# Entering the feed-forward sublayers: transposing four quarters and forming the three sums from the transposed blocks

## The chip, the core and the metric

The kernel runs on one core of one Trainium2 chip. The metric is the device time of one execution in microseconds. Three runs of the kernel before took 2835.72, 2828.82 and 2835.14 us, median 2835.14 us; a fourth execution was profiled.

## The reference, cut to what matters

A trunk of two layers on 512 tokens of width 1024; each layer is feed-forward, mixer (gated DeltaNet in the first, Mamba-2 in the second), cross-attention, feed-forward. So there are four feed-forward sublayers. What each does with the residual stream `h`:

```python
def swiglu(x, w_in, w_out):
    gate, up = jnp.split(x @ w_in, 2, axis=-1)
    return (jax.nn.silu(gate) * up) @ w_out

u = swiglu(rms_norm(h, g[0, 0]), ffn_w_in[l, 0], ffn_w_out[l, 0])
h = h + MACARON_W * rms_norm(u, g[0, 1])
```

All data are float32, `w_in` is 1024 x 5632, `w_out` 2816 x 1024.

## The kernel before, in words

**Arithmetic.** Every float32 operand of a product is split in two rounded parts, hi and lo (ScalarE casts hi, VectorE subtracts to get lo), and `mm3` (L143 to L145) issues three products: hi by hi, hi by lo, lo by hi. Features lie on partitions, tokens on the free axis, so what enters a sublayer must be transposed.

**The first product of a feed-forward** saves products by sums of quarters (seven instead of eight). With tokens cut in halves of 256 and features in halves of 512, the input is A11, A12 (first half of the tokens) and A21, A22. The products need A11, A12, A22 and S1 = A21 + A22, S2 = S1 - A11, S3 = A11 - A21, S4 = A12 - S2, each transposed and split in hi and lo. A11, A12, S1 and A22 go to the tiles `xh`/`xl`, the others to `s2h`/`s2l`, `s3h`/`s3l`, `s4h`/`s4l`.

**`FFN.enter(i, ...)`** (L365) does this for one block of 128 tokens, i = 0 to 3. VectorE scales the block with its reciprocal root and the gains (L373, two instructions of 128x512, into `u`). `put` then sends one 128x512 piece through TensorE's transpose (L379, four instructions of 128x128 into one PSUM bank), ScalarE casts hi out of the bank (L381) and VectorE subtracts lo (L382). For i = 0 and 1 there are two such pieces. For i = 2 and 3 there are five: x's second half for A22, and the sums `xs` (S1, L391), S2 (L394), S4 (L396) and S3 (L393), which VectorE forms from `u`, with tokens on partitions, before each is transposed. So one entry has 2 + 2 + 5 + 5 = 14 pieces and 56 transposes. The banks are those of tag "c", of which there are two (the first entry, at the kernel's start, also uses "s").

**What stands around it.** For the sublayer in front, `tail` finishes a block of 128 tokens, `post` (L225 multiplies by the gains `gbc`, L202 to L204 form the reciprocal root `rcol`, L230 adds to `h`), then `sumsq` (L196) and `enter` follow. After the last block's tail, `head` issues the products of the first four weight tiles with A11 and A12 (4 x 24 = 96 products of 128x256), which need only i = 0 and 1. `FFN.rest` goes on with `plain(0)` and `plain(1)`: two loads into `raw` (L440), T14 = their differences (L454, into the space of `h`), its split, products of the weights with S1, then of T14 with A22. `pair(2)` and on take the seven products; L489 and L492/L493 are its first operations on a `raw`. Tiles named `raw` have three buffers, so a load waits until an earlier `raw` has been read. `warm` loads ScalarE's table for Silu (L210).

**Order of the work.** The program is written out in plain order, and a scheduler orders each engine's instructions by priorities (`later` shifts them by a table, `LATER`); each engine then runs its own list strictly in that order. The list of each engine is known when the kernel is built.

The first entry stands at the kernel's start; the entry of FFN 1 comes after the first cross-attention, that of FFN 2 after FFN 1, that of FFN 3 after the second cross-attention. The instructions around the entries of FFN 1 and FFN 3 have the same order on VectorE and ScalarE.

Of the kernel before, what the change touches and what calls it, by code (L numbers as in the profile page):

```python
# [52 lines left out]
def prio(name):  # L53
    def wrap(f):
        def g(self, *a, **k):
            with getattr(self, "t", self).later(name):
                return f(self, *a, **k)
        return g
    return wrap
# [275 lines left out]
class FFN:  # L335
# [29 lines left out]
    @prio('ff_enter')  # L365
    def enter(self, i, ss, tag):

        t, nc = self.t, self.t.nc
        r = t.rcol(ss)
        x = t.u[:, i, :]  # L370
        a, b = slice(0, T), slice(T, D)
        for s in (a, b):
            nc.vector.scalar_tensor_tensor(x[:, s], t.h[:, i, s], r[:, 0:1], self.pg[:, s], op0=ALU.mult, op1=ALU.mult)  # L373
        ts = slice(i % 2 * P, i % 2 * P + P)

        def put(src, dst):
            ps = t.bank(tag)
            for k in range(4):
                nc.tensor.transpose(ps[:, k * P:k * P + P], src[:, k * P:k * P + P], t.cst(C_ID))  # L379
            p = ps.rearrange("p (k t) -> p k t", k=4)  # L380
            nc.scalar.copy(dst[0][:, :, ts], p)  # L381
            nc.vector.tensor_sub(dst[1][:, :, ts], p, dst[0][:, :, ts])  # L382

        if i < 2:
            put(x[:, a], self.A11)
            put(x[:, b], self.A12)
        else:
            y = t.u[:, i - 2, :]
            put(x[:, b], self.A22)
            s1 = t.nt.tile([P, T], F32, name="xs", bufs=2)  # L390
            nc.vector.tensor_add(s1, x[:, a], x[:, b])  # L391
            put(s1, self.S1)
            nc.vector.tensor_sub(x[:, a], y[:, a], x[:, a])  # L393
            nc.vector.tensor_sub(y[:, a], s1, y[:, a])  # L394
            put(y[:, a], self.S2)
            nc.vector.tensor_sub(y[:, b], y[:, b], y[:, a])  # L396
            put(y[:, b], self.S4)
            put(x[:, a], self.S3)
# [931 lines left out]
def run(t, phases, n0=0):  # L1330
# [17 lines left out]
    with ExitStack() as c:  # L1348
        if hasattr(phases[0], "gains"):
            phases[0].gains(c, n0)  # L1350
            phases[0].sums()
        for i in range(NT):
            if i:
                t.load(i)
            ss = t.nt.tile([P, 2], F32, name="ssh", bufs=2)
            for f in range(2):
                t.sumsq(t.h[:, i, f * T:f * T + T], ss[:, f:f + 1], f and i < 2)
            enter(i, n0, phases[0], ss, "cscc"[i])
            if i % 2:
                phases[0].head(i // 2, i == 1)  # L1360
        t.load_rest()
    for j, ph in enumerate(phases):
        n = n0 + j
        nxt = phases[j + 1] if j + 1 < len(phases) else None
        with ExitStack() as c:
            if hasattr(nxt, "gains"):
                nxt.gains(c, n + 1)
            ph.open(c)
            t.post_gain(n)
            t.warm(AF.Silu, t.xh[:, KB - 1, T - 1:T])  # L1370
            ph.rest()
            if hasattr(nxt, "sums"):
                nxt.sums()
            for i in range(NT):
                t.tail(ph, i)
                if i == 0:
                    t.warm(AF.Sqrt, t.ssu[:, 0, 0:1])
                if i == NT - 1:
                    c.close()
                    if nxt:  # L1380
                        nxt.head(0)
                ss = t.post(i, nxt)
                if nxt:
                    enter(i, n + 1, nxt, ss)
                else:
                    for f in range(2):
                        fs = slice(f * T, f * T + T)
                        nc.sync.dma_start(out=t.ap["out"][i * P:(i + 1) * P, fs], in_=t.h[:, i, fs])
            if nxt:
                nxt.head(1)  # L1390
# [41 lines left out]
```

## Time and profile before

| | |
|---|---|
| median of three runs | 2835.14 us (2828.82 to 2835.72) |
| the profiled execution, its own time | 2833.57 us |
| its span, first to last instruction | 2831.8 us |
| PE (TensorE) busy | 2785.9 us, 98% |
| DVE (VectorE) busy | 2071.3 us, 73% |
| ACT (ScalarE) busy | 1512.9 us, 53% |
| transposes of the entries (L379) | 224 instructions |
| granted TensorE clock, mean | 0.993 |

In the profile PE is TensorE's products (a transpose is one of them), DVE is VectorE, ACT ScalarE, SP the engine that issues the transfers. A row of a timeline has the start, the busy time, the engine, the line, the tile written and those read, and in brackets how long the engine had been idle and what released it. Busy times of neighbouring rows overlap, because engines are pipelined, so what an instruction takes from its engine is the distance between starts. The granted clock is a share of 2.4 GHz.

### The profile page before, as it was taken

What the parts mean: (1) busy time and instruction counts of PE and PEld (TensorE: products, weight loads), DVE (VectorE), ACT (ScalarE), POOL (GpSimd) and SP (SyncE); (2) the same over time, 40 slices, a digit from 0 to 9 for tenths busy, and PEclk for the clock granted to TensorE, in tenths of its full rate; (3) what the DMA queues carried; (4) which work ended last, traced back from release to release, by engine and by line L of the source; (5) the groups of instructions that cost most, each with busy time, mean ns of one, the idle gap of its engine ahead of it and who ended that gap; (6) DMA issues with size and microseconds to landing.
All of it is one profiled execution on the core that took longest, in us unless ns stands there. A gap on an engine that the chain in (4) does not pass through costs nothing.

```text
span 2831.8 us, 45624 instructions
## 1 busy us (share of the span) xinstructions
PE 2785.9 (98%) x17648; PEld 2453.5 (87%) x17648; DVE 2071.3 (73%) x4057; ACT 1512.9 (53%) x2814; POOL 124.5 (4%) x141
## 2 busy tenths in 40 slices
PE   8999999999999999999999999999999999999998
PEld 7999987788888887999988999888888888799997
DVE  8887777767666564887778887777667766588776
ACT  5444477666575574544445444576554656454433
POOL 0000001000000000000000000003212200000000
PEclk9999999999999999999999999999999999999999
DMA  6333433232323432433343332433233363233233
GB/s 215 106 105 105 160 111 103 62 100 81 94 71 121 168 116 73 143 100 102 97 156 127 98 112 90 152 121 108 85 104 106 103 217 112 75 113 112 93 109 105
DMA packets 125913, 320.71 MB, mean 113 GB/s; under 512 B 27472, under 2 KB 46672, under 8 KB 125184
## 3 DMA queue, kind: packets, MB, share of 16 engines
q1 hardware_dynamic: 125696, 317.80, 34.6%
q8 instruction: 139, 2.28, 0.3%
q14 instruction: 78, 0.64, 0.1%
HBM read 293.01 MB, written 24.74 MB: 112 GB/s over the span
## 4 chain that ended last, share of the span: by engine, by line
PE 86%; DVE 7%; ACT 3%; DMA 2%; issue 1%; SPq 0%; DVEq 0%; POOL 0%; ACTq 0%; POOLq 0%
PE ps_a L143 16%; PE ps_a L144 16%; PE ps_a L145 16%; PE ps_s L144 4%; PE ps_s L145 4%; PE ps_s L143 4%; PE ps_c L143 2%; PE ps_c L145 2%; PE ps_c L144 2%; PE ps_f L145 2%; PE ps_f L144 2%; PE ps_f L143 2%; DVE wlo L130 1%; PE ps_c L1068 1%; PE ps_s L1237 1%
## 5 line engine op out<-in xcount | busy, mean ns | idle before, releaser
L143 PE MATMUL ps_a<-xh,whi 128*128 128x256 f32 (+1 forms) x2368 | 754.8, 321 | 2.0 <-ACT xh L381 1.7
L144 PE MATMUL ps_a<-xl,whi 128*128 128x256 f32 (+1 forms) x2368 | 755.4, 320 | 0.1
L145 PE MATMUL ps_a<-xh,wlo 128*128 128x256 f32 (+1 forms) x2368 | 752.3, 319 | 0.0
L143 PEld LDWEIGHTS ps_a<-xh,whi 128*128 128x128 f32 x2368 | 453.5, 192 | 30.3 <-ACT xh L381 2.6
L144 PEld LDWEIGHTS ps_a<-xl,whi 128*128 128x128 f32 x2368 | 455.0, 192 | 26.4 <-DVE xl L382 0.5
L145 PEld LDWEIGHTS ps_a<-xh,wlo 128*128 128x128 f32 x2368 | 454.4, 192 | 23.9
L130 DVE TENSOR_TENSOR wlo<-raw,whi 128x1024 fp32r<-128x1024 f32 x278 | 339.8, 1224 | 159.2 <-ACT whi L129 157.2
L129 ACT CAST whi<-raw 128x1024 fp32r<-128x1024 f32 x278 | 289.1, 1043 | 224.5 <-PE ps_a L144 139.1
L137 ACT CAST whi<-h 128x1024 fp32r<-128x1024 f32 x168 | 175.6, 1048 | 204.3 <-PE ps_a L144 150.3
L138 DVE TENSOR_TENSOR wlo<-h,whi 128x1024 fp32r<-128x1024 f32 x168 | 205.3, 1224 | 88.7 <-ACT whi L137 87.7
L492 ACT CAST bh<-raw 128x512 fp32r<-128x512 f32 x80 | 49.7, 621 | 169.0 <-DMA raw<-ffn_in 140.5
L144 PE MATMUL ps_s<-wlo,hhi 128*128 128x512 f32 x352 | 138.0, 392 | 0.0
L143 PE MATMUL ps_s<-whi,hhi 128*128 128x512 f32 x352 | 137.8, 392 | 0.0
L145 PE MATMUL ps_s<-whi,hlo 128*128 128x512 f32 x352 | 137.2, 390 | 0.0
L143 PE MATMUL ps_c<-whi,hhi 128*128 128x512 f32 x288 | 112.0, 389 | 0.0
L144 PE MATMUL ps_c<-wlo,hhi 128*128 128x512 f32 x288 | 112.0, 389 | 0.0
L145 PE MATMUL ps_c<-whi,hlo 128*128 128x512 f32 x288 | 112.0, 389 | 0.0
L137 ACT CAST whi<-raw 128x1024 fp32r<-128x1024 f32 x80 | 84.0, 1051 | 50.3 <-PE ps_c L145 39.0
L485 DVE TENSOR_TENSOR h<-raw 128x512 f32<-128x512 f32 x80 | 55.1, 689 | 72.1 <-DMA raw<-ffn_in 69.4
L138 DVE TENSOR_TENSOR wlo<-raw,whi 128x1024 fp32r<-128x1024 f32 x80 | 97.4, 1218 | 8.7 <-ACT whi L137 8.7
L512 ACT ACTIVATE h<-h 128x512 f32<-128x512 f32 x80 | 50.6, 633 | 84.3 <-DVE h L509 84.1
L468 ACT CAST hhi<-h 128x512 fp32r<-128x512 f32 x88 | 54.8, 622 | 71.7 <-DVE h L513 43.6
(423 smaller groups left out, 6635.4 us busy)
## 6 DMA issues: line engine op xcount, KB each, us to landing
raw<-ffn_in SPq DMA_DIRECT2D x192, 512.0 KB, 4.2
raw<-ffn_out SPq DMA_DIRECT2D x88, 512.0 KB, 3.5
raw<-dn_in SPq DMA_DIRECT2D x48, 512.0 KB, 3.5
raw<-ssd_in SPq DMA_DIRECT2D x32, 512.0 KB, 3.5
hd<-h SPq DMA_DIRECT2D x24, 512.0 KB, 3.1
h<-hd SPq DMA_DIRECT2D x24, 512.0 KB, 4.2
raw<-dn_out SPq DMA_DIRECT2D x16, 512.0 KB, 3.6
raw<-xa_k SPq DMA_DIRECT2D x16, 512.0 KB, 3.9
```

The lines of the kernel that those rows point to most:

```text
L129: nc.scalar.copy(hi[:, :n], raw[:, :n])
L130: nc.vector.tensor_sub(lo[:, :n], raw[:, :n], hi[:, :n])
L137: nc.scalar.copy(hi, raw)
L138: nc.vector.tensor_sub(lo, raw, hi)
L143: mm(ps, lhs[0], rhs[0], start=first, stop=False)
L144: mm(ps, lhs[0], rhs[1], start=False, stop=False)
L145: mm(ps, lhs[1], rhs[0], start=False, stop=last)
L468: self.t.nc.scalar.copy(hi, x)
L485: sub(T1, u[:, a], g[:, a])
L492: nc.scalar.copy(b22[0], u[:, b])
L512: nc.scalar.activation(gt, gt, AF.Silu)
L1068: nc.tensor.matmul(py[:, e * 64:e * 64 + 64], st["gp"][e][:, c, :], st["xt"][:, c, e * 64:e * 64 + 64], start=True, stop=True)
```

## The change

`put` is cut in two: `turn` transposes one piece into a bank, `put` casts and subtracts from whatever it is given. For i = 0 and 1, ScalarE also copies each transposed piece back into `u`. For i = 2 and 3 only A22 and A21 are transposed, one behind the other; ScalarE copies A21 back into `u`, and the sums are formed from the transposed blocks and split from SBUF.

```diff
-        def put(src, dst):
+        def turn(src):
             ps = t.bank(tag)
             for k in range(4):
                 nc.tensor.transpose(ps[:, k * P:k * P + P], src[:, k * P:k * P + P], t.cst(C_ID))
-            p = ps.rearrange("p (k t) -> p k t", k=4)
+            return ps
+
+        def put(src, dst):
+            p = src.rearrange("p (k t) -> p k t", k=4)
             nc.scalar.copy(dst[0][:, :, ts], p)
             nc.vector.tensor_sub(dst[1][:, :, ts], p, dst[0][:, :, ts])
 
         if i < 2:
-            put(x[:, a], self.A11)
-            put(x[:, b], self.A12)
+            for s, dst in ((a, self.A11), (b, self.A12)):
+                ps = turn(x[:, s])
+                put(ps, dst)
+                nc.scalar.copy(x[:, s], ps)
         else:
             y = t.u[:, i - 2, :]
-            put(x[:, b], self.A22)
+            p22, p21 = turn(x[:, b]), turn(x[:, a])
+            put(p22, self.A22)
+            nc.scalar.copy(x[:, a], p21)
             s1 = t.nt.tile([P, T], F32, name="xs", bufs=2)
-            nc.vector.tensor_add(s1, x[:, a], x[:, b])
+            nc.vector.tensor_add(s1, p22, x[:, a])
             put(s1, self.S1)
             nc.vector.tensor_sub(x[:, a], y[:, a], x[:, a])
             nc.vector.tensor_sub(y[:, a], s1, y[:, a])
             put(y[:, a], self.S2)
```

In the changed file the cast of `put` is L384, its subtraction L385, the copies L391 (i = 0, 1) and L396 (A21), the sums L398 (S1), L400 (S3), L401 (S2), L403 (S4); lines behind `enter` are 7 higher (L454 is L461, L489 is L496, L492 is L499, L440 is L447). Outside the entries every engine's list is as before. Three places in the entry of FFN 1:

**TensorE**, from the last products of `head` (into `ps_s`) to the first of `plain(0)` (`ps_a<-xh` with four single rows is S1). Before:

```order
L144 MATMUL ps_s<-xl,whi 128x256
L379 MATMUL ps_c<-const,u 128x128 x4
L145 MATMUL ps_s<-xh,wlo 128x256
L143 MATMUL ps_a<-xh,whi 128x256 x2
L143 MATMUL ps_s<-xh,whi 128x256 x2
L379 MATMUL ps_c<-const,u 128x128 x4
L144 MATMUL ps_a<-xl,whi 128x256
L145 MATMUL ps_a<-xh,wlo 128x256
L379 MATMUL ps_c<-const,u 128x128 x4
```

Now:

```order
L144 MATMUL ps_s<-xl,whi 128x256
L145 MATMUL ps_s<-xh,wlo 128x256
L379 MATMUL ps_c<-const,u 128x128 x8
L143 MATMUL ps_a<-xh,whi 128x256 x2
L143 MATMUL ps_s<-xh,whi 128x256 x2
L144 MATMUL ps_a<-xl,whi 128x256
L145 MATMUL ps_a<-xh,wlo 128x256
```

Before, the transposes of i = 3 are spread over the last products of `head` and the first of `plain(0)`, and 14 rows stand between S1's and the product that needs them. Now all eight stand behind the last product of `head`, and the next instruction needs S1.

**VectorE**, from i = 2's last sums to i = 3's scaling (L373; `s4l` and `s3l` are i = 2's, `rcol`, L230 and what follows i = 3's). Before:

```order
L382 TENSOR_TENSOR s4l<-ps_c,s4h 128x4x128
L204 RECIPROCAL rcol<-rcol 128x1
L138 TENSOR_TENSOR wlo<-h,whi 128x1024
L382 TENSOR_TENSOR s3l<-ps_c,s3h 128x4x128
L230 SCALAR_TENSOR_TENSOR h<-u,rcol,h 128x512 x2
L454 TENSOR_TENSOR h<-raw 128x512 x2
L202 TENSOR_TENSOR rcol<-ssh 128x1
L204 RECIPROCAL rcol<-rcol 128x1
L373 SCALAR_TENSOR_TENSOR u<-h,rcol,pg 128x512 x2
```

Now:

```order
L385 TENSOR_TENSOR s4l<-u,s4h 128x4x128
L202 TENSOR_TENSOR rcol<-ssu 128x1
L461 TENSOR_TENSOR h<-raw 128x512
L204 RECIPROCAL rcol<-rcol 128x1
L461 TENSOR_TENSOR h<-raw 128x512
L230 SCALAR_TENSOR_TENSOR h<-u,rcol,h 128x512 x2
L202 TENSOR_TENSOR rcol<-ssh 128x1
L496 TENSOR_TENSOR h<-raw 128x512
L204 RECIPROCAL rcol<-rcol 128x1
L373 SCALAR_TENSOR_TENSOR u<-h,rcol,pg 128x512 x2
```

The two subtractions on the loads of `plain(1)` (L454, now L461) moved ahead of L230, and `pair(2)`'s first subtraction on a load (L489, now L496) moved from behind i = 3's scaling to ahead of it.

**ScalarE and SP** in the same entry; on ScalarE from i = 3's `rcol` to the cast of S1. Before:

```order
L203 ACTIVATE rcol<-rcol,eps 128x1
L381 CAST xh<-ps_c 128x4x128
L210 ACT_TABLE_LOAD
L210 ACTIVATE warm<-xh 128x1
L381 CAST xh<-ps_c 128x4x128
```

Now:

```order
L203 ACTIVATE rcol<-rcol,eps 128x1
L499 CAST bh<-raw 128x512
L384 CAST xh<-ps_c 128x4x128
L396 COPY u<-ps_c 128x512
L210 ACT_TABLE_LOAD
L210 ACTIVATE warm<-xh 128x1
L384 CAST xh<-xs 128x4x128
```

On SP the loads of `plain` and `pair`, before:

```order
L440 DMA raw<-ffn_in 128x1024 x4
L214 DMA gbc<-post 128x1024
L1339 DMA hd<-h 128x1024
L440 DMA raw<-ffn_in 128x1024
L356 DMA pg<-pre 128x1024
L128 DMA raw<-ffn_out 128x1024
```

Now:

```order
L447 DMA raw<-ffn_in 128x1024 x4
L214 DMA gbc<-post 128x1024
L447 DMA raw<-ffn_in 128x1024
L128 DMA raw<-ffn_out 128x1024
L1346 DMA hd<-h 128x1024
L356 DMA pg<-pre 128x1024
```

The cast of S1 now has the copy of A21 and the table load between it and A22's cast, and `pair(2)`'s cast on a load (L499) in front of both; on SP the spill of `h` stands behind `pair(2)`'s load and the first load of `w_out`.

## Rows read from the trace of the kernel before

**Rows 1.** The page: busy time of the engines, and the chain that ended last.
```profile
PE 2785.9 (98%) x17648; PEld 2453.5 (87%) x17648; DVE 2071.3 (73%) x4057; ACT 1512.9 (53%) x2814; POOL 124.5 (4%) x141
...
PE 86%; DVE 7%; ACT 3%; DMA 2%; issue 1%; SPq 0%; DVEq 0%; POOL 0%; ACTq 0%; POOLq 0%
```

**Rows 2.** Timeline of PE, one piece's transposes among products, entry of FFN 2.
```profile
1490.92 0.28 PE L143 MATMUL ps_a<-xh,whi 128*128 128x256 f32 x1
1491.04 0.60 PE L379 MATMUL ps_c<-const,u 128*128 128x128 f32 x4
1491.40 0.36 PE L144 MATMUL ps_a<-xl,whi 128*128 128x256 f32 x1
1491.60 0.28 PE L145 MATMUL ps_a<-xh,wlo 128*128 128x256 f32 x1
```

**Rows 3.** Timeline of PE, entry of FFN 1, from the first product of head.
```profile
1134.86 0.28 PE L143 MATMUL ps_a<-xh,whi 128*128 128x256 f32 x1
...
1147.25 0.63 PE L379 MATMUL ps_c<-const,u 128*128 128x128 f32 x4 [0.42 <-DVE u L373]
...
1150.56 0.49 PE L143 MATMUL ps_a<-xh,whi 128*128 128x256 f32 x2
...
1151.68 0.66 PE L379 MATMUL ps_c<-const,u 128*128 128x128 f32 x4 [0.40 <-DVE xl L382]
...
1152.78 0.36 PE L143 MATMUL ps_a<-xh,whi 128*128 128x256 f32 x1
```

**Rows 4.** Timeline of DVE, the same entry, from plain(0)'s second L454 to i = 3's L373.
```profile
1134.50 0.69 DVE L454 TENSOR_TENSOR h<-raw 128x512 f32<-128x512 f32 x1 [0.72 <-DMA raw<-ffn_in]
...
1140.31 1.20 DVE L138 TENSOR_TENSOR wlo<-h,whi 128x1024 fp32r<-128x1024 f32 x1
1141.43 0.68 DVE L382 TENSOR_TENSOR s3l<-ps_c,s3h 128x512 fp32r<-128x512 f32 x1
1142.03 1.40 DVE L230 SCALAR_TENSOR_TENSOR h<-u,rcol,h 128x512 f32<-128x512 f32 x2
...
1145.69 1.42 DVE L373 SCALAR_TENSOR_TENSOR u<-h,rcol,pg 128x512 f32<-128x512 f32 x2
```

**Rows 5.** Timeline of ACT, the same entry, i = 3's casts of A22 and S1.
```profile
1147.91 0.59 ACT L381 CAST xh<-ps_c 128x512 fp32r<-128x512 f32 x1 [2.46 <-PE ps_c L379]
1148.52 1.28 ACT L210 ACT_TABLE_LOAD   x1
...
1149.92 0.57 ACT L381 CAST xh<-ps_c 128x512 fp32r<-128x512 f32 x1
```

**Rows 6.** A load of pair(2) in FFN 2's entry: issue, landing; the slowest 512 KB loads' median.
```profile
1502.44 0.33 SPq L440 DMA_DIRECT2D raw<-ffn_in  x1
...
1506.66 0.62 ACT L492 CAST bh<-raw 128x512 fp32r<-128x512 f32 x1 [0.86 <-DMA raw<-ffn_in]
...
h<-x SPq DMA_DIRECT2D x4, 512.0 KB, 5.6
```

**Rows 7.** Timeline of PE, entry of FFN 2, i = 3.
```profile
1504.55 0.63 PE L379 MATMUL ps_c<-const,u 128*128 128x128 f32 x4 [3.40 <-DVE u L373]
...
1507.82 0.80 PE L143 MATMUL ps_a<-xh,whi 128*128 128x256 f32 x2 [1.74 <-ACT xh L381]
...
1510.01 0.41 PE L145 MATMUL ps_a<-xh,wlo 128*128 128x256 f32 x1
1510.22 0.41 PE L143 MATMUL ps_a<-xh,whi 128*128 128x256 f32 x1
...
1513.43 0.28 PE L143 MATMUL ps_a<-xh,whi 128*128 128x256 f32 x1
```

**Rows 8.** A stretch of PE: us, busy (instructions), granted clock, DMA share, GB/s.
```profile
1508.00:1514.00 6.00, 6.00 (x34) 0.63 0.00 0
```

**Rows 9.** Timelines of DVE and PE, the first entry.
```profile
14.29 1.42 DVE L373 SCALAR_TENSOR_TENSOR u<-h,rcol,pg 128x512 f32<-128x512 f32 x2
...
33.95 0.50 PE L143 MATMUL ps_a<-xh,whi 128*128 128x256 f32 x2
```

## The prediction

> **What bounds the kernel now.** The page comes first: PE is busy for 98% of the span and the chain that ended last lies on PE for 86% [rows 1]. So a product less is time less, as long as PE does not end up waiting. That is asked where the change acts, in the four entries, about 20 us each. The order of reading there: the timeline of PE (what a transpose costs, where PE waits), then the chain that ends PE's wait, followed back through ScalarE and VectorE, then the clock.
>
> One piece's four transposes, among products that start 0.12 us apart, push the next product from 0.12 to 0.36 us behind and the one after it from 0.12 to 0.20 or so: 0.44 us for a piece [rows 2]. In the entry of FFN 1, `head`'s 96 products begin at 1134.86, S1's first product starts at 1150.56 [rows 3]. Of these 15.7 us the products take 96 x 0.12 = 11.5, six pieces' transposes 6 x 0.44 = 2.6, waits on VectorE most of the rest. In the same 15.7 us block i = 3 goes through `post`, `sumsq` and `enter`, on VectorE and ScalarE, and becomes S1 only at its end: S1's cast starts at 1149.92 and takes 0.57 [rows 5], PE takes S1 at once. So here **two things end together, PE's list and the chain of block i = 3**, and the transposes fill time in which PE would have waited. In the entry of FFN 2 the chain is already the longer one: PE waits 3.40 and 1.74 us in it, and its clock falls [rows 7, 8].
>
> **The change, part by part.**
>
> *Removed:* 6 of 14 pieces in an entry, 24 in all, 24 x 0.44 = 10.6 us of PE. Per entry the three sums of i = 2 and the three of i = 3, so 6 x 0.44 = 2.6 us, and all of them stand in or just behind the stretch in which the chain of i = 3 runs.
>
> *Added:* six copies of 128x512 from PSUM on ScalarE per entry, 0.5 us from start to start like a cast [rows 5]; casts from SBUF instead of PSUM (bounds 0.57 and 0.62 us, L381 and L492 [rows 5, 6]: no difference that matters). VectorE has as many instructions as before, 0.60 us from start to start [rows 4]. Off the chain all this is free, because ScalarE is busy for 53% only [rows 1].
>
> *Moved, and here the price lies.* I walk the queues in their new order with the distances of the rows.
>
> Entry of FFN 1. VectorE before: from L454 at 1134.50 to i = 3's L230 at 1142.03 [rows 4]. Now between the same two stand thirteen instructions of 0.60 (that L454 included), one L138 of 1.1 and two small ones of 0.1, 9.1 us: L230 at 1143.6. The two extra ones are `plain(1)`'s L461s, which moved ahead; the first of them, which ends at 1142.9, also gives its `raw` buffer back, and only then SP can issue `pair(2)`'s load. The same load in the next entry landed 4.2 us after its issue [rows 6]: here at 1147.1. VectorE's L496 waits for it, and **behind L496 stand i = 3's reciprocal and its L373**, so L373 starts at 1147.1 + 0.6 + 0.1 = 1147.8, not 1145.69 [rows 4], and the transposes at 1149.35, not 1147.25 [rows 3]. PE, with three pieces fewer of i = 2 and no waits, is through `head` at 1134.9 + 11.5 = 1146.4 and waits 3.0 us. After the transposes (8 of them, 0.75 us) ScalarE casts A22 0.66 us behind their start, as before [rows 3, 5], copies A21 (0.5), loads the Silu table (1.4 up to the next row [rows 5]) and casts S1 (0.6): 1150.0 + 0.5 + 0.5 + 1.4 + 0.6 = 1153.0. The sum on VectorE is done under the table load. So S1's product starts at 1153.0 instead of 1150.56, **2.4 us later**, behind a second wait of 2.9 us.
>
> From there PE gets back what the old list had behind S1: two pieces (0.9) and a wait of 0.40 [rows 3]. The twentieth product behind S1 came at 1154.3 (the one at 1152.78 is the seventh [rows 3], thirteen more at 0.12). At full clock it would now come at 1153.0 + 19 x 0.12 + 0.2 (S1's lo) = 1155.5: +1.2. But two waits of 3.40 and 1.74 us, with 0.7 us of transposes between, brought the clock to a mean of 0.63 in FFN 2's entry, that is to 1.2 of 2.4 GHz for about 4.4 of 6 us [rows 7, 8]; products then start 0.21 apart [rows 7]. With waits of 3.0 and 2.9 I take the same here: 1153.0 + 19 x 0.21 = 1157.0, **+2.7**. The Trainium skill (TensorE: Matmul & The Clock Gate, section on HAM oscillation) says that waits between bursts of products let the clock fall and that the next burst starts at half rate; the trace agrees in FFN 2's entry, and by that rule the entry costs 2.7, without it 1.2.
>
> Entry of FFN 3: the same order on VectorE and ScalarE, +2.7.
>
> Entry of FFN 2. Two copies of i = 1 (1.0) and an L461 (0.6) now stand ahead of i = 2's reciprocal; i = 2's L373 comes 1.3 later, the L461 that frees the load's buffer 0.7 later, so the load lands at 1507.3 instead of 1506.66 [rows 6]. ScalarE's L499 waits for it, and the copy of A21, the table load and S1's cast stand behind: 1507.3 + 0.5 + 0.5 + 1.4 + 0.6 = 1510.3 instead of 1507.82 [rows 7]. Both are at the low clock. The twentieth product came at 1513.7 (the one at 1513.43 is the eighteenth [rows 7]), with three pieces ahead of it; now at 1510.3 + 19 x 0.21 = 1514.3: **+0.6**.
>
> First entry. Two copies stand ahead of the first weights' cast, whose subtraction stands ahead of i = 1's reciprocal on VectorE: L373 1.0 later than 14.29, PE's start with it. Through VectorE's longer list S1 is ready at 35.0 instead of 33.95 [rows 9], and three pieces behind it (1.3) come back: **-0.2**.
>
> Sum: -0.2 + 2.7 + 0.6 + 2.7 = **+5.8 us**. Against the profiled execution's own time, 2833.6, that is 2839.4; the median of the runs shown is 1.6 higher, so 2841.0 as a median. Bounds: if the clock does not fall in FFN 1 and 3, -3.0 (then +2.8); if the load lands at once L373 still waits for the chain through ScalarE, -0.4 in three entries; if it lands in 5.6 us, the slowest of the loads of its size [rows 6], +1.4 in three entries, +10.0 in all. I take 4.2, from the same load in the nearest entry.
>
> **The rivals.** About 0.3%, 8.5 us, is what a measurement of this kernel can tell from no change.
>
> *The chain is no longer than before* (its waits hide each other): S1 at its old times, and only the pieces behind S1 come back: 0.9 + 0.4 in FFN 1 and 3, 1.3 in the first entry, three pieces in FFN 2, two of them at half clock, 2.2: -6.1, 2829.0. For it speaks that ScalarE and VectorE have idle time in between; against it that VectorE's list ahead of L230 is counted longer by two instructions and has hardly a gap [rows 4].
>
> *PE is the bound throughout* and all 24 pieces come off: -10.6, 2824.5. For it: 98% [rows 1]. Against: the waits of rows 7, and that S1's transposes were ready early only because they were spread. It decides if S1 is ready before `head`'s 96 products end.
>
> *The loads land late.* On SP `pair(2)`'s load is now followed at once by a load of `w_out`, where the spill of `h` stood; two loads share the engines and hold up VectorE in front of L496. With 5.6 us: +10.0, 2845.1, over 0.3%; it decides from 0.9 us more than the 4.2 on.
>
> **How the numbers follow.** The forecast (+0.5 to +8.5) 0.58, the unlengthened chain 0.13, the full gain 0.07, late loads or a longer chain beyond +8.5 0.22. So faster 0.07, same 0.71, slower 0.22. The likeliest time is 2841.0; the range reaches down past the second case (2829.0) and up past the third rival (2845.1), each by a little for the spread of the runs shown: 2828 to 2849.
>
> **What would show it.** Right: 128 transposes, no wait of PE for anything but the entries; in FFN 1 and 3 a wait of about 3 us on L373 ahead of eight transposes, a second of about 3 us on the cast of S1 (L384), then products 0.21 apart; VectorE idle ahead of L496 on a load; PE's busy time lower and its idle time higher by more. Wrong: transposes of i = 3 that start at the old time after the tail, clock at 1.00 in FFN 1, or PE's idle time unchanged, which would mean that the 24 pieces were paid out.

## The result, and the profile after

The changed kernel took **2852.2 us** in the median of its runs (2849.1 to 2854.6), the kernel before 2834.3 beside it: ratio **1.0066, 95% interval 1.0048 to 1.0085**, so 13.6 to 24.1 us slower. Forecast were 2841.0 and a range of 2828 to 2849. The profiled execution took 2854.3 us, its span 2852.5: 20.7 over the span of before.

The page after, busy time [against rows 1]:

```profile
PE 2786.5 (98%) x17552; PEld 2452.9 (86%) x17552; DVE 2073.1 (73%) x4057; ACT 1527.1 (54%) x2838; POOL 128.0 (4%) x141
```

PE runs 96 instructions less, which are the 24 pieces, and is busy for as long as before: what the pieces gave back, instructions at the low clock took (the mean granted clock went from 0.993 to 0.987). PE's idle time rose by 20.1 us. Much of it shows in the group of PE's transposes (after the bar: busy time and mean, then the idle time ahead and what ended it), before:

```profile
L379 PE MATMUL ps_c<-const,u 128*128 128x128 f32 x184 | 29.8, 289 | 16.7 <-DVE u L373 14.8 <-DVE u L394 0.9 <-DVE xl L382 0.8
```

and after:

```profile
L379 PE MATMUL ps_c<-const,u 128*128 128x128 f32 x120 | 19.9, 308 | 26.4 <-DVE u L373 26.2
```

Before, this group waited 14.8 us for L373, and now 26.2. The wait of the first product of S1 (L143) for its cast, 1.7 us in one place before, is 8.2 in three.

**Where the 20.7 us arose.** Lines behind `enter` are 7 higher now, but the instructions of ScalarE are the same ones, so their shift between the two traces can be read. Two of them ahead of and behind the entry of FFN 1, before:

```profile
1093.99 1.28 ACT L210 ACT_TABLE_LOAD   x1
...
1232.67 0.63 ACT L512 ACTIVATE h<-h 128x512 f32<-128x512 f32 x1 [1.11 <-DVE h L509]
```

and the same two after:

```profile
1104.79 1.28 ACT L210 ACT_TABLE_LOAD   x1
...
1247.91 0.64 ACT L519 ACTIVATE h<-h 128x512 f32<-128x512 f32 x1 [1.11 <-DVE h L516]
```

The shift is 10.80 ahead and 15.24 behind: this entry cost 4.4 us. An entry's cost is this difference: the shift behind it less the shift ahead of it. With medians over all ScalarE instructions of a stretch ahead and behind, every run of this study gives such a row (us, against the profile of before; "elsewhere" is the shift at the end less the four entries):

| kernel | first | FFN 1 | FFN 2 | FFN 3 | sum | elsewhere |
|---|---|---|---|---|---|---|
| the change | 1.85 | 4.45 | 0.98 | 5.66 | 12.9 | 7.8 |
| the change, once more | 1.81 | 5.51 | -0.01 | 6.11 | 13.4 | 10.4 |
| first entry only | 1.66 | -0.01 | 0.02 | -0.54 | 1.1 | 2.0 |
| FFN 1 to 3 only | -0.18 | 5.66 | 1.34 | 5.68 | 12.5 | -4.4 |
| L496 tied | 0.64 | 3.93 | 0.13 | 3.45 | 8.2 | 12.7 |
| fillers | 1.02 | 3.37 | -2.12 | 3.76 | 6.0 | 10.1 |
| i = 0 and 2 only | 2.81 | 6.07 | -0.91 | 6.32 | 14.3 | 0.8 |
| i = 1 and 3 only | 4.39 | -0.34 | 1.28 | -0.39 | 4.9 | 0.1 |
| L496 tied, short chain | 0.11 | 1.37 | -0.44 | 1.00 | 2.0 | -3.4 |
| the same with fillers | 0.01 | 1.82 | -0.26 | 0.69 | 2.3 | 2.6 |
| the same, i = 2's rest removed | 4.52 | -0.87 | -0.10 | -1.44 | 2.1 | 1.6 |
| what paid, together | -0.52 | -1.20 | -0.33 | -1.93 | -4.0 | 0.4 |

Entries that a kernel left as they were cost -0.5 to 0.0, so this measure is good to about half a us. The entries of the change itself differ by up to 1.1 us between its two profiles, so smaller differences between two kernels say little. "Elsewhere" isn't a term of the entries. In the change, 5.8 of its 7.8 us arise at 858 to 868 us, deep in DeltaNet, where PE's granted clock was at its lower level (columns: busy us of PE, PEld, DVE, ACT and POOL with their instructions, granted clock, DMA share, GB/s):

```profile
860.00:870.00 10.00, 10.00 (x58) 8.08 (x57) 3.72 (x20) 6.57 (x23) 0.00 (x0) 0.50 0.01 2
```

and before:

```profile
860.00:870.00 10.00, 10.00 (x59) 8.75 (x59) 8.87 (x28) 6.51 (x14) 1.27 (x2) 1.00 0.64 173
```

Such stretches come and go in all kernels of the table. If the lost clock is added up over rows of 10 us from 450 to 1085 us (10 x (1 - clock) each), it is 13.7 us in the profile of before, 20.5 in that of the change, 27.2 with L496 tied, 6.8 with the short chain: 6.8, 13.5 and -6.9 against before, where the table has 7.8, 12.7 and -3.4. In the other kernels of the table the two numbers also agree within 4 us (8.4 against 10.4 in the second profile of the change).

**Inside the entry of FFN 1.** Take the shift ahead of the entry, 10.8, off these times to compare them with [rows 3 to 5]; times so reduced are called times on the old scale below. VectorE:

```profile
1154.20 1.41 DVE L230 SCALAR_TENSOR_TENSOR h<-u,rcol,h 128x512 f32<-128x512 f32 x2
1156.56 0.16 DVE L202 TENSOR_TENSOR rcol<-ssh 128x1 f32<-128x1 f32 x1 [0.94 <-ACT junk L196]
1159.37 0.69 DVE L496 TENSOR_TENSOR h<-raw 128x512 f32<-128x512 f32 x1 [2.66 <-DMA raw<-ffn_in]
1159.98 0.16 DVE L204 RECIPROCAL rcol<-rcol 128x1 f32<-128x1 f32 x1
1160.17 1.41 DVE L373 SCALAR_TENSOR_TENSOR u<-h,rcol,pg 128x512 f32<-128x512 f32 x2
```

L230 comes 1.4 us later than before (1143.4 against 1142.03). Then VectorE stands 2.66 us idle at L496 for its load, with the last block's L204 and L373 behind it. SP's queue, to see when that load was issued:

```profile
1153.65 0.33 SPq L447 DMA_DIRECT2D raw<-ffn_in  x1
1154.31 0.33 SPq L128 DMA_DIRECT2D raw<-ffn_out  x1
1155.64 0.33 SPq L1346 DMA_DIRECT2D hd<-h  x1
```

From the issue at 1153.65 to L496 at 1159.37 are 5.7 us, with a second load and the spill of `h` (`hd`) directly behind, and the load of the gains `gbc` (L214, at 1152.38) directly ahead. ScalarE:

```profile
1157.84 0.28 ACT L203 ACTIVATE rcol<-rcol,eps 128x1 f32<-128x1 f32 x1
...
1162.40 0.59 ACT L384 CAST xh<-ps_c 128x512 fp32r<-128x512 f32 x1 [2.41 <-PE ps_c L379]
1163.13 0.59 ACT L396 COPY u<-ps_c 128x512 f32<-128x512 f32 x1
1163.73 1.28 ACT L210 ACT_TABLE_LOAD   x1
1165.13 0.60 ACT L384 CAST xh<-xs 128x512 fp32r<-128x512 f32 x1
```

The square root (L203) had been done at 1158.1, so L496 cost 1.9 us of the chain. The four rows below it on ScalarE are A22's cast, A21's copy, the table and S1's cast, in the order that the prediction walked. PE:

```profile
1145.51 0.27 PE L143 MATMUL ps_a<-xh,whi 128*128 128x256 f32 x1
...
1156.89 0.28 PE L145 MATMUL ps_s<-xh,wlo 128*128 128x256 f32 x1
1161.73 1.36 PE L379 MATMUL ps_c<-const,u 128*128 128x128 f32 x8 [4.56 <-DVE u L373]
1165.79 0.80 PE L143 MATMUL ps_a<-xh,whi 128*128 128x256 f32 x2 [2.70 <-ACT xh L384]
...
1167.02 0.41 PE L145 MATMUL ps_a<-xh,wlo 128*128 128x256 f32 x1
1167.23 0.41 PE L143 MATMUL ps_a<-xh,whi 128*128 128x256 f32 x1
...
1169.29 0.28 PE L145 MATMUL ps_a<-xh,wlo 128*128 128x256 f32 x1
1169.41 0.28 PE L143 MATMUL ps_a<-xh,whi 128*128 128x256 f32 x1
```

`head`'s 96 products run through (11.5 us), then PE waits 4.56 and 2.70 us, with eight transposes between. Products behind S1 start 0.21 apart until 1169.3, then 0.12. The clock of the same stretch:

```profile
1158.00:1160.00 2.00, 0.00 (x0) 0.00 (x0) 0.63 (x2) 0.74 (x2) 0.00 (x0) 1.00 1.00 397
...
1162.00:1164.00 2.00, 1.09 (x8) 0.69 (x6) 1.14 (x3) 1.44 (x3) 0.00 (x0) 0.59 0.66 225
...
1166.00:1168.00 2.00, 2.00 (x10) 2.00 (x11) 2.00 (x4) 1.40 (x3) 0.00 (x0) 0.50 0.00 0
...
1170.00:1172.00 2.00, 2.00 (x19) 2.00 (x18) 1.71 (x2) 1.28 (x2) 0.00 (x0) 1.00 0.00 0
```

PE did nothing at 1158 to 1160, the clock fell behind that, to 1.2 of 2.4 GHz, and rose again once S1's products ran. Before, it stayed at 1.00 in this entry, also where S1's products begin:

```profile
1150.00:1152.00 2.00, 1.60 (x13) 1.37 (x13) 2.00 (x4) 1.50 (x4) 0.00 (x0) 1.00 0.79 303
```

In FFN 2 and FFN 3 PE shows the same two waits [against rows 7]:

```profile
1519.99 1.94 PE L379 MATMUL ps_c<-const,u 128*128 128x128 f32 x8 [4.84 <-DVE u L373]
1524.78 0.79 PE L143 MATMUL ps_a<-xh,whi 128*128 128x256 f32 x2 [2.85 <-ACT xh L384]
...
2505.21 1.94 PE L379 MATMUL ps_c<-const,u 128*128 128x128 f32 x8 [4.51 <-DVE u L373]
2509.85 0.80 PE L143 MATMUL ps_a<-xh,whi 128*128 128x256 f32 x2 [2.70 <-ACT xh L384]
```

The first entry [against rows 9]. PE began block i = 1 so before the change:

```profile
15.10 1.97 PE L379 MATMUL ps_s<-const,u 128*128 128x128 f32 x8 [4.35 <-DVE u L373]
```

Now it starts 1.34 us later, then waits for the last block and, in `pair(2)`, for the split of a load (L500):

```profile
16.44 1.97 PE L379 MATMUL ps_s<-const,u 128*128 128x128 f32 x8 [5.33 <-DVE u L373]
...
31.81 1.06 PE L379 MATMUL ps_c<-const,u 128*128 128x128 f32 x8 [1.64 <-DVE u L373]
...
52.27 0.39 PE L145 MATMUL ps_a<-s4h,bl 128*128 128x256 f32 x1 [0.96 <-DVE bl L500]
```

Before, PE had neither of the last two waits.

### The profile page after: what moved, and what is told of

It reads as the page before. It is cut to its first block, busy times and chain, and to the rows that moved or that the text cites. A ratio compares the mean times of both kernels' runs of the same rounds, so it can differ in the third digit from the quotient of the medians.

```text
span 2852.5 us, 45440 instructions
## 1 busy us (share of the span) xinstructions
PE 2786.5 (98%) x17552; PEld 2452.9 (86%) x17552; DVE 2073.1 (73%) x4057; ACT 1527.1 (54%) x2838; POOL 128.0 (4%) x141
## 4 chain that ended last, share of the span: by engine, by line
PE 86%; DVE 7%; DMA 3%; ACT 2%; issue 1%; POOL 0%; SPq 0%; DVEq 0%; ACTq 0%
PE ps_a L143 16%; PE ps_a L145 16%; PE ps_a L144 16%; PE ps_s L144 4%; PE ps_s L143 4%; PE ps_s L145 4%; PE ps_c L145 2%; PE ps_c L143 2%; PE ps_c L144 2%; PE ps_f L145 2%; PE ps_f L144 2%; PE ps_f L143 2%; DMA raw<-ffn_in 1%; DVE wlo L130 1%; PE ps_c L1075 1%
## 5 line engine op out<-in xcount | busy, mean ns | idle before, releaser
L143 PE MATMUL ps_a<-xh,whi 128*128 128x256 f32 (+1 forms) x2368 | 757.6, 322 | 8.3 <-ACT xh L384 8.2
L143 PEld LDWEIGHTS ps_a<-xh,whi 128*128 128x128 f32 x2368 | 456.0, 193 | 37.5 <-ACT xh L384 9.7
L499 ACT CAST bh<-raw 128x512 fp32r<-128x512 f32 x80 | 49.8, 622 | 174.8 <-DMA raw<-ffn_in 135.5
L143 PE MATMUL ps_s<-whi,hhi 128*128 128x512 f32 x352 | 137.8, 392 | 0.0
L143 PE MATMUL ps_c<-whi,hhi 128*128 128x512 f32 x288 | 112.0, 389 | 0.0
L492 DVE TENSOR_TENSOR h<-raw 128x512 f32<-128x512 f32 x80 | 55.2, 690 | 75.1 <-DMA raw<-ffn_in 73.4
```

Of the source, the lines that this page charges most:

```text
L143: mm(ps, lhs[0], rhs[0], start=first, stop=False)
L492: sub(T1, u[:, a], g[:, a])
L499: nc.scalar.copy(b22[0], u[:, b])
```

## The experiments

**One part of the entries at a time.** The new and the old way side by side in `enter`, chosen by

```diff
+        new = self.idx == 0
+        if not new:
...
+            return
```

> The new way of forming the sums in the first entry alone; the entries of FFN 1, 2 and 3 as before. In the profiles of the changed kernel and of before the first entry cost 1.85 us, FFN 1's 4.3, FFN 2's 1.0, FFN 3's 5.65 (12.8 in all), and 7.8 us arose elsewhere, 5.8 of them in one stretch of low granted clock at 858 to 868 us, far from any entry. Theory A (the cost lies in the entries, and what arose elsewhere is no part of the mechanism): +1.9 us against the kernel before, about 2836, granted clock 0.993. Theory B (the new first entry shifts what follows, and the rest of the kernel pays): +1.9 + 7.8 = +9.7, about 2844, with a low clock near 860.

Measured: ratio 1.0004 (0.9985 to 1.0023), and 1.1 us in the entries. 9.7 us would be 1.0034, outside the interval: theory B falls, although this profile too has a low clock at 860 to 870.

With `new = self.idx > 0`:

> The first entry as before, the new way in FFN 1, 2 and 3. Up to 1104 us this is the kernel before, instruction for instruction. Theory A: +4.3 + 1.0 + 5.65 = +11.0, about 2845, and whether the stretch of low clock near 860 appears is chance (then about 5.8 more). Theory B: +11.0 and never a low clock near 860, which the shift by the first entry had caused; together with the run of the first entry alone the two differences make up the +18 of the changed kernel.

Measured: ratio 1.0037 (1.0020 to 1.0054), 5.7 to 15.3 us; by the trace 12.7 in the three entries. The stretch of low clock at 850 to 870 us is there without the new first entry: that entry isn't its cause.

**The subtraction in front of the last block**

```diff
+        if n == 2:
+            nc.vector.tensor_copy(T3[:, 0:1], self.S1[1][:, 0, 255:256])
         sub(T3, u[:, b], u[:, a])
```

> The changed kernel with pair(2)'s subtraction for T3 (L496) tied behind the low half of S1, by a tiny copy of 128x1, so that it can't stand ahead of the last block's reciprocal and L373 on VectorE. In the profile of the changed kernel L496 waited 2.66 us for its load in FFN 1 and 2.31 in FFN 3 with the reciprocal ready behind it. Theory A (this wait is a term of the chain): L373 and S1's first product 1.9 us earlier in FFN 1 and 3, little in FFN 2, so -3 to -4 against the changed kernel, about 2848.5. Theory C (the chain through ScalarE and the clock set S1 anyway): within 1 us of the changed kernel, about 2852.

Ratio to before 1.0043 (1.0026 to 1.0061). VectorE in FFN 1 (its shift ahead of the entry is 14.4 here):

```profile
1161.50 0.16 DVE L204 RECIPROCAL rcol<-rcol 128x1 f32<-128x1 f32 x1 [1.25 <-ACT rcol L203]
1161.69 1.42 DVE L373 SCALAR_TENSOR_TENSOR u<-h,rcol,pg 128x512 f32<-128x512 f32 x2
```

and PE:

```profile
1163.26 1.93 PE L379 MATMUL ps_c<-const,u 128*128 128x128 f32 x8 [2.56 <-DVE u L373]
1167.88 0.80 PE L143 MATMUL ps_a<-xh,whi 128*128 128x256 f32 x2 [2.70 <-ACT xh L384]
```

L373 starts at 1147.3 on the old scale instead of 1149.4: 2 us, as theory A has it, and PE's first wait falls from 4.56 to 2.56. The entries cost 4.8 less than in the change (5.3 against its second profile), of it 2.2 to 2.7 in FFN 3 and 1.2 in the first entry, where I had expected none; in FFN 1 only 0.5 to 1.6, since the clock fell there all the same, and stayed low until 5.5 us behind S1's first product, in the change 3.5. What is left of the first wait comes from ScalarE: L204 waits for L203 (1161.18), which stands behind L216 (1160.22, the halving of the gains).

**The clock.** `fill` issues products of A11 or A22 with themselves, at a late priority, into banks that the transposes and S1's product overwrite, so they fill the waits and change no result:

```diff
+            p22, p21 = turn(x[:, b], 36 * k), turn(x[:, a], k)
...
+        if n == 0 and self.idx:
+            self.fill(ps[0][:, 256:], self.A22, 20)
         for i in range(2):
             self.product(ps[i][:, 256:], self.part(ws[i], 0), self.S1, True, False)
```

> The changed kernel with 37 filler products ahead of the last block's transposes and 20 ahead of S1's first product, in FFN 1, 2 and 3; their sums are thrown away. PE waited 4.5 to 4.8 and 2.7 to 2.9 us there, and its granted clock was 0.50 from the end of the first wait until 3.6 (FFN 1), 6.7 (FFN 2) and 4.1 us (FFN 3) behind S1's first product. Theory A (the waits let the clock fall, and the products behind S1 pay): clock 1.00 in the entries, S1's products 0.12 apart and not 0.21, half of those times back, 1.8 + 3.3 + 2.0 = -7 against the changed kernel, about 2845; S1's first product not earlier by more than 0.5 us. Rival (the low clock has another cause): the clock stays low, and no time comes back or some is lost.

Ratio to before 1.0045 (1.0030 to 1.0060). The three entries by stretches:

```profile
1157.00:1171.00 14.00, 13.17 (x106) 12.53 (x106) 8.86 (x15) 8.47 (x15) 0.00 (x0) 1.00 0.38 137
1514.00:1532.00 18.00, 17.15 (x138) 16.29 (x137) 16.18 (x26) 11.64 (x21) 0.00 (x0) 1.00 0.27 89
2497.00:2511.00 14.00, 13.17 (x106) 12.48 (x105) 8.89 (x15) 8.32 (x15) 0.00 (x0) 1.00 0.28 98
```

The clock stays at 1.00 in all three, and they cost 6.1 less than in the change (6.6 against its second profile); expected were 7. So with the waits filled the clock doesn't fall, and that is worth about 2 us an entry. The Trainium skill (TensorE: Matmul & The Clock Gate, section on HAM oscillation) has it that waits between bursts bring the clock down; these rows agree, with the reverse: filled waits keep it up.

**Which half of the rows.** `new = i % 2 == 0` and `new = i % 2 == 1`, in all four entries:

> The new way for the blocks i = 0 and 2 alone; i = 1 and 3 as before, in all four entries. In VectorE's list of FFN 1 and 3 the subtraction for T3 still stands ahead of the last block's reciprocal. An entry's cost is read as the shift, against the kernel before, of the work behind it less that of the work ahead of it. Theory A (the longer list of i = 2 and the late load are the larger half): PE waits about 4 us ahead of the last block's transposes in FFN 1 and 3, and each costs 3 to 4 us, FFN 2 about 0. Theory D (what costs is the last block's own chain, through the copy of A21 and the sum): at most 0.5 us each.

> The new way for the blocks i = 1 and 3 alone; i = 0 and 2 as before. VectorE's list up to the last block's L373 is that of before, and the subtraction for T3 stands behind the sum for S1. Theory A: no wait of PE over 0.5 us ahead of the eight transposes, then one of 2.7 us on S1's cast, clock 1.00 in FFN 1 and 3; these two cost 1 to 1.5 us each. Theory D: 3 us or more each.

With i = 0 and 2 alone (single execution, 2848.7 us), VectorE and PE in FFN 1:

```profile
1152.87 0.69 DVE L522 TENSOR_TENSOR h<-raw 128x512 f32<-128x512 f32 x1 [2.77 <-DMA raw<-ffn_in]
```

```profile
1155.23 1.09 PE L390 MATMUL ps_c<-const,u 128*128 128x128 f32 x4 [5.11 <-DVE u L373]
```

L522 is L496 here. With i = 1 and 3 alone (single execution, 2838.6 us), PE:

```profile
1152.54 1.06 PE L379 MATMUL ps_c<-const,u 128*128 128x128 f32 x8 [0.41 <-DVE u L373]
...
1156.35 0.50 PE L143 MATMUL ps_a<-xh,whi 128*128 128x256 f32 x2 [0.96 <-ACT xh L384]
```

Theory D falls: the longer chain of i = 3 costs nothing in FFN 1 and 3 (-0.3 and -0.4), because L373 is nearly on time (1146.1 on the old scale, before 1145.69), PE takes the transposes ahead of `head`'s last 15 products and these cover all but 0.96 us of the chain. The half of i = 2 carries all of it, and more (6.1 and 6.3). Theory A had the side right and both sizes wrong. In the first entry it is the other way round (4.4 for i = 1 and 3, 2.8 for i = 0 and 2), which I hadn't expected; the clock fell there in both (0.88 at 40 to 50 us, 0.83 at 30 to 40), while it stayed at 1.00 in the change, so the halves don't add up to the whole.

**The chain of the last block, shortened,** on top of the tied L496:

```diff
-            p22, p21 = turn(x[:, b]), turn(x[:, a])
-            put(p22, self.A22)
+            p21 = turn(x[:, a])
             nc.scalar.copy(x[:, a], p21)
+            p22 = turn(x[:, b])
...
             put(s1, self.S1)
+            put(p22, self.A22)
...
-            t.warm(AF.Silu, t.xh[:, KB - 1, T - 1:T])
+            k = 4 if isinstance(ph, FFN) else KB
+            t.warm(AF.Silu, t.xh[:, k - 1, T - 1:T])
```

> The kernel with L496 tied behind S1's low half, and besides A21 turned and copied ahead of A22, S1's cast ahead of A22's, and the load of the Silu table put behind S1's cast. In the profile of that kernel PE waited 2.56 us on L373 and 2.70 on S1's cast in FFN 1. Theory A (the rest is the chain from the transposes to S1): the second wait falls by the cast (0.5) and what of the table load was on the path (0.7), to 1.2 to 1.7 us, and an entry costs 1.0 to 1.5 us less than with L496 tied alone (3.9, 0.1 and 3.5). Rival (VectorE, not ScalarE, sets S1): the second wait stays over 2.4 us.

Single execution, 2832.2 us. VectorE and PE in FFN 1:

```profile
1144.20 1.42 DVE L373 SCALAR_TENSOR_TENSOR u<-h,rcol,pg 128x512 f32<-128x512 f32 x2
```

```profile
1145.10 1.29 PE L379 MATMUL ps_c<-const,u 128*128 128x128 f32 x8 [1.61 <-DVE u L373]
1147.89 0.80 PE L143 MATMUL ps_a<-xh,whi 128*128 128x256 f32 x2 [1.50 <-ACT xh L384]
```

The second wait falls from 2.70 to 1.50, inside the bounds; FFN 1 and 3 cost 2.5 less than with L496 tied alone, more than expected, because the first wait fell too (2.56 to 1.61): A21 is the half of `u` that the first of L373's two instructions writes, so PE starts 0.90 us behind L373's start instead of 1.57. The three edits weren't run one by one. The first entry is level with before again.

The same with 27 fillers ahead of the last block's transposes:

> The kernel of the shortened chain with L496 tied, and 27 filler products ahead of the last block's transposes in FFN 1, 2 and 3 (their sums are thrown away). Theory A: clock 1.00 in all three entries; costs against before of about +1, -2.5 and +1 us, and the whole kernel level with before (within 0.3%). Rival (the fillers are too few for the second wait): the clock falls behind it, and entries cost as much as without them.

Ratio 1.0013 (0.9994 to 1.0031). The whole is level, as expected, but not for the reason: in FFN 1 the clock fell behind the second wait, which has no fillers (to 0.50 at 1158 to 1160 us), and FFN 2, where it fell too (0.66 at 1510 to 1520), gave back 0.3 instead of 2.5. There the rival was right. In FFN 3 the clock stayed at 1.00 behind a second wait of the same 1.50 us, and the entry cost 0.7.

**Once more the change itself**

> The changed kernel itself once more, beside the kernel before, in more executions. Its first profile had +12.9 us in the entries and +7.8 elsewhere; in the runs so far what arose elsewhere lay between -4 and +13, in kernels that are the same there. Theory A (elsewhere is chance): the entries again 1.9, 4 to 6, 1 and 5.7, elsewhere another value, and the median of many runs about 13 us over that of before, ratio 1.0045. Theory B (elsewhere is part of the change): +18 again, ratio 1.0065, with a low clock near 860 us and +7 to 8 elsewhere.

Ratio 1.0049 (1.0029 to 1.0068), that is 8 to 19 us; the median of its executions is 2855.5 against 2836.8, with three at 2838 to 2844 and eight at 2853 to 2861. The entries repeat: 13.4. Elsewhere is 10.4, with the low clock at 860 to 880 and one more at 710 to 730. So 13 us of the change are the entries. Both theories' ratios lie in the interval, and a low clock near 860 is there again, as theory B has it; but the kernel with fillers, which is the same at that place, shows none there. Whether the changed kernel meets these stretches more often than others do, or by chance in both profiles, these runs don't settle.

**What is left of i = 2's list**

```diff
-            self.nc.scalar.mul(self.gbc, self.gbc, 0.5)
+            self.nc.gpsimd.tensor_scalar(self.gbc, self.gbc, 0.5, None, op0=ALU.mult)
...
+        if n == 1 and self.idx:
+            nc.vector.tensor_copy(self.T14[:, 0:1], t.h[:, 3, D - 1:D])
```

> The kernel of the shortened chain with L496 tied, and besides one of plain(1)'s two subtractions for T14 tied behind the last block's L230 on VectorE (0.6 us), and the halving of the gains (L216, 1.0 us) moved from ScalarE, where it stood between the last block's squares and its square root, to GpSimd. Theory A (these two are what is left of the longer list of i = 2): L373 1.2 us earlier, S1 0.7 to 1.2 earlier (pair(2)'s cast may hold ScalarE), FFN 1 and 3 cost 0 to 0.6 us instead of 1.4 and 1.0. Rival (the loads' landing now sets it): no change of more than 0.3.

Single execution, 2837.3 us. FFN 1 and 3 now cost less than before the change, -0.9 and -1.4, beyond what was expected, with the whole new way in place; VectorE and PE in FFN 1 (shift ahead 5.3):

```profile
1151.52 2.28 DVE L373 SCALAR_TENSOR_TENSOR u<-h,rcol,pg 128x512 f32<-128x512 f32 x2
```

```profile
1153.28 0.63 PE L379 MATMUL ps_c<-const,u 128*128 128x128 f32 x4 [2.34 <-DVE u L373]
1156.10 0.50 PE L143 MATMUL ps_a<-xh,whi 128*128 128x256 f32 x2 [1.04 <-ACT xh L384]
```

The second wait is 1.04, the clock 1.00. But in FFN 1 S1 isn't earlier, as theory A had it: its first product starts at 1150.8 on the old scale, as with the shortened chain alone. L373 starts 0.9 earlier there, yet its two instructions take 2.28 us instead of 1.42, while GpSimd runs its multiplication (1151.55 to 1154.32). What FFN 1 gained is the clock, which had been 0.50 at 1148 to 1152 us with the shortened chain; why it stays up here, with six of `head`'s products between the two waits, wasn't tested. In FFN 3 S1 is 1.2 us earlier, as expected. The first entry pays 4.5: there GpSimd's halving of the gains, or the new order around it, let the clock fall to 0.83 at 30 to 50 us; I didn't separate these.

**What paid, together**

```diff
+        new = (self.idx in (1, 3) and i % 2 == 1) or self.idx == 2
```

with L496 tied, the shortened chain, and 24 fillers and one in FFN 2 alone:

> The parts that paid, together: first entry as before; FFN 1 and 3 with the new way for i = 1 and 3 alone and the shortened chain; FFN 2 with the new way for all, the shortened chain and 25 filler products. Theory A: 0, about -1.3, about -1, about -1.3 in the four entries, -3 to -4 us in all: faster than before by the profile, by less than a measurement can tell (ratio 0.9985 to 0.9990). Rival (the shortened chain brings VectorE's order of the changed kernel back): 1 us or more over before in FFN 1 and 3.

Ratio 0.9988 (0.9972 to 1.0003), 2832.7 us against 2836.8. By the trace its entries are 4.0 us faster, as expected; PE waits 0.48 and 0.49 us for L373 in FFN 1 and 3, and the clock is 1.00 there. It is the fastest version by its profile (span 2828.2), but the interval holds no change.

## Why the prediction was wrong in size

*Right.* Slower, for the reason given: PE's list and the chain of i = 3 end together, and the change lengthens the chain. VectorE's order with L496 ahead of L204 and L373, the two waits, the eight transposes in a row and products 0.21 apart are all there. On the old scale: L230 forecast for 1143.6, measured 1143.4; issue of the load 1142.9, measured 1142.85; second wait 2.9, measured 2.70; FFN 2 +0.6, measured 1.0, 0.0 and 1.3. One sign failed: PE's busy time was to be lower, and it stayed (2785.9 before, 2786.5 after).

*Wrong, the term that was mis-sized:* "I take 4.2, from the same load in the nearest entry". The load took 5.7 us to L496 in FFN 1 and 5.4 in FFN 3 (issue 2497.48, L496 at 2502.85). That is the rival "the loads land late", with its own price of 5.6: L373 at 1149.4 instead of 1147.8, PE's first wait 4.56 instead of 3.0. By that rival FFN 1 and 3 cost 4.1 each; measured were 4.45 to 6.1 in three profiles. I had read the load of `w_out` that stands behind on SP and given the case a chance; but that reason isn't shown: in FFN 2's entry, from which the 4.2 comes, the load of `w_out` stands as close behind (issued at 1503.11, the other at 1502.44). What differs is `gbc`, 1.3 us ahead in FFN 1 and 3 and not near in FFN 2. In all profiles in which `gbc` stands so, the load took 4.3 to 5.9 us up to its first reader, in FFN 2's entries 3.5 to 4.8; which neighbour slows it wasn't tested. The tied L496 shows that this term is real: 2 us off L373.

*Wrong, a smaller term:* from the transposes to S1 I had 3.65 us (1149.35 to 1153.0). The clock fell before the transposes were through: the eight took 1.36 us in FFN 1 and 1.94 in FFN 3 instead of 0.75, and S1 came 4.06 and 4.64 us behind their start. In FFN 3 L230 was also 2.0 late and not 1.6.

*Wrong, the first entry:* -0.2 forecast, 1.8 measured twice. PE's start was forecast 1.0 later and came 1.34 later; S1's first product, forecast for 35.0, came at 35.63. The three pieces behind S1 did come back: PE's list was 2.9 us late ahead of S1 and 0.6 late at 40 us. The step that failed is that nothing was counted behind that: in `pair(2)` PE waits 0.96 us on L500, a wait that it didn't have before, and from there on it is 1.85 late. With the shortened chain, where this wait is gone, the entry costs 0.0 to 0.1.

*Wrong, the range.* The forecast put what arises outside the entries at nothing, and took "a little" for the spread, from three runs that lay 7 us apart. Of the 14.9 us between its +5.8 and the 20.7 of the profiles, 7.1 lie in the entries and 7.8 elsewhere. With the entries alone (12.9 to 13.4) the time would have been 2847 to 2848.5 us, inside the range; the stretches of low clock far from the entries carried it out. Why both profiles of the change have more of them than the profile of before stays open. Some 27 executions of the kernel before, beside the first experiments, lay between 2826.9 and 2849.4.

*The rivals below.* Neither the unlengthened chain (-6.1) nor PE as the bound (-10.6) came: PE's waits on L373 ahead of the transposes grew from 14.8 to 26.2 us, those on S1's cast from 1.7 to 8.2.

## What to carry to other kernels

Where an engine's list is ordered ahead of time, look for an instruction that waits for a load and stands in front of a chain that ends a stretch; price it at the slowest landing that the trace shows for such a load with others around it, not at the nearest. Removing work from an engine that is 98% busy was worth nearly nothing here in a stretch whose end is a chain on other engines; and the idle time that it left cost the clock on top. Change such a place piece by piece: in FFN 1 and 3 one half of this edit was worth 0.3 us and the other cost 6, each in a single execution.

## What the runs showed of the hardware that I had not expected

PE's granted clock falls in DeltaNet also where PE is counted busy without a gap: 0.50 at 860 to 870 us with 10.00 of 10 us busy, in some executions and not in others. In the change one such stretch is worth 5.8 us, as much as an entry of this study. The time of whole runs goes with the clock: among 22 executions of the kernel before, the fastest (2828.7 us) had a mean of 0.996 and the slowest (2848.2 us) 0.987. For an edit of a few us the shift of the same instructions between two traces tells more than the time of the kernel: it repeated to about half a us in entries that were left alone.

Fillers ahead of both waits held the clock at 1.00 in all three entries. Fillers ahead of the first wait alone did not hold it in FFN 1, and it stayed up in FFN 3, behind a second wait of 1.50 us in both: the length of a wait alone doesn't tell whether the clock falls.
